# A decoder layer on one core: the whole program in stated TensorE order, norms and token forms as steps between products, inverse root through Ln and Exp

## The chip, the cores and the metric

The kernel runs on 1 core of one Trainium2 chip. A core has five engines that run side by side, each working through its own queue in order: TensorE (PE; matmul), VectorE (DVE), ScalarE (ACT), GpSimd (POOL) and SyncE (SP), which here issues the DMA transfers. The metric is the device time of one launch in microseconds. Time before: 3101.36 us, the median of 3 runs (3099.22 to 3108.59).

## The reference

One step of one decoder layer, width 1024, for 1024 prompt tokens and 8 x 4 sample tokens, 1056 tokens in all. Its norms, where this change works, are one function:

```python
def _rmsnorm(x, g):
    xf = x.astype(jnp.float32)
    y = xf * lax.rsqrt(jnp.mean(xf * xf, axis=-1, keepdims=True) + EPS)
    return (y * g.astype(jnp.float32)).astype(x.dtype)

h = x + 0.5 * _swiglu(_rmsnorm(x, g_ffn1), w_ffn1_in, w_ffn1_out)
u = _rmsnorm(h, g_mix)
# mixer on u: dilated window attention, gated linear attention, cross-attention into
# 256 memory tokens, whose keys and values are
kv = _rmsnorm(mem, g_mem) @ w_mem_kv
h = h + jnp.sum(gates * br, axis=2) @ w_out
h = h + 0.5 * _swiglu(_rmsnorm(h, g_ffn2), w_ffn2_in, w_ffn2_out)
y = _rmsnorm(h, g_final)
```

The reference also returns the new keys and values, the memory keys and values and the states of the linear attention.

## The kernel before, in words

**Products.** Tokens lie along the free dimension, features on the 128 partitions: a [1024, 1056] activation is eight tiles of 128 x 1056. Each fp32 operand is split into a high and a low part, and a product takes three matmuls per tile of the contracted dimension, high by high, high by low, low by high (`product`, L180 to L182). `split` (L186, L187) makes the high part by a cast on ScalarE and the low part by a subtraction on VectorE or GpSimd; `weights` (L166, L167) does the same for weights, in two rotating buffers each (whi, wlo).

**The SwiGLUs.** The hidden width 2816 is worked in 22 blocks of 128. In a block the pair of input products (two weight matrices by two token halves) goes as 7 products in place of 8, with sums and differences of the weights (`weight_forms`) and of the tokens (class `Forms`). The 1056 tokens are four chunks of 264 (c = 0 to 3), in two halves p = 0, 1. Per half and per row of forms i = 0 to 3, `Forms.make` scales four pieces by gain and inverse root (L316), makes two subtractions on GpSimd (L318, L319) and two on VectorE (L320, L321), and splits the results into the tiles xs. `pair_products` then runs j = 0 to 6 for both halves, each product 12 matmuls of 264 columns (4 rows by 3). The token forms are made once, ahead of the first block, for all 22 blocks. The output product (`out_product`) sums over blocks of 4 or 3 hidden tiles: for each of 8 output tiles and 3 chunks of 352 tokens a product of 12 or 9 matmuls, added onto h by VectorE (L554). In the last such block the chunk loop is the outer one, so that the norm of a finished chunk can begin.

**Norms.** Per chunk ScalarE squares (L208) and GpSimd adds (L209); a matmul with ones (L235) sums over partitions and gives one sum per token, on partitions. `rsqrt` (L220 to L227, 13 VectorE operations: a first guess from the bits and three Newton steps) makes rqy. `spread` (L245) brings it back to a row on every partition by matmuls with the identity; `normed` (L255) or the forms (L316) use it.

**The first norm.** `x_features` reads nine tiles of rows, sums their squares on ScalarE and VectorE, transposes them (L435) and copies them out (L439, L441). **Memory.** After the first output block of the first SwiGLU comes `mem_kv`: the 256 memory rows' squares (L475), root, scaling (L481), 16 transposes (L488), then the products for keys and values.

**What sets the order.** A scheduler places the instructions of each engine's queue by its own timing model and by priorities; the norms' sums and spreads have high priority. Only the mixer between the two SwiGLUs runs in a manual TensorE order, the order of the code.

## Time and profile before

| what | value |
|---|---|
| median of 3 runs | 3101.36 us (3099.22 to 3108.59) |
| the profiled execution | 3088.57 us |
| its span, first to last instruction | 3086.8 us |
| TensorE busy | 2917.7 us, 95% |
| VectorE, ScalarE, GpSimd busy | 48%, 33%, 32% |
| mean granted TensorE clock | 0.968 of full |

Busy shares are over the whole span. A table of stretches shows the same for a part of it, a timeline lists single instructions with start and duration in us, and a bracket at the end of its row gives the idle time of the engine ahead of the instruction and what ended it. Matmuls overlap, so that the duration of one is longer than the step from one to the next; the step is read from the evacuations behind products.

### The profile page before, as it was taken

The page shows a single profiled execution, that of the slowest core. Times are in us where ns is not written, and L with a number is a line of the kernel's source. Part 1 is how long each engine was busy: PE and PEld are TensorE (multiplying, and loading weights), DVE is VectorE, ACT ScalarE, POOL GpSimd, SP SyncE. Part 2 cuts the span into 40 slices and gives each one's busy share as a digit, 9 for nine tenths or more (in the row PEclk, how much of TensorE's full clock was granted, in tenths as well). Part 3 has the DMA queues.
Part 4 walks back from the last instruction along what each step waited for, and adds up shares of the span by engine and source line. Part 5 has one row for each costly group of instructions (what it writes and reads, how often), then busy time and mean ns, then how long its engine had stood idle before and what let it go on. Part 6 is the DMA issues. An engine that isn't in the chain of part 4 may idle for free. (4 is left out here: it accounts for less than half of the span.)

```text
span 3086.8 us, 51261 instructions
## 1 busy us (share of the span) xinstructions
PE 2917.7 (95%) x20747; PEld 2843.8 (92%) x20747; DVE 1488.5 (48%) x2746; ACT 1005.5 (33%) x2014; POOL 994.8 (32%) x815
## 2 busy tenths in 40 slices
PE   4999999999999999999898998999995999999998
PEld 3999999899999999988797997999995999999997
DVE  8444444554623446656665551222257444444545
ACT  4333333221435443332232421221224333333212
POOL 5333332010400114546456350222436333332100
PEclk6999999999999999999999999999997999999999
DMA  4222224431311224657566564221221222225312
GB/s 141 76 82 77 84 73 164 145 126 55 106 51 48 71 55 133 174 156 199 143 193 176 169 197 114 70 66 42 98 78 61 83 81 73 83 77 196 104 50 89
DMA packets 438883, 328.65 MB, mean 106 GB/s; under 512 B 34131, under 2 KB 396597, under 8 KB 438645
## 3 DMA queue, kind: packets, MB, share of 16 engines
q1 hardware_dynamic: 438578, 325.35, 34.7%
q8 instruction: 163, 2.67, 0.4%
q14 instruction: 76, 0.61, 0.1%
q10 hardware_dynamic: 66, 0.02, 0.0%
HBM read 264.69 MB, written 60.60 MB: 105 GB/s over the span
## 5 line engine op out<-in xcount | busy, mean ns | idle before, releaser
L180 PE MATMUL acc<-xh,whi 128*128 128x352 f32 x1776 | 594.9, 335 | 0.0
L182 PE MATMUL acc<-xh,wlo 128*128 128x352 f32 x1776 | 583.0, 328 | 8.4 <-DVE wlo L167 8.4
L181 PE MATMUL acc<-xl,whi 128*128 128x352 f32 x1776 | 581.2, 327 | 0.0
L182 PEld LDWEIGHTS acc<-xh,wlo 128*128 128x128 f32 x1776 | 340.7, 192 | 13.9 <-DVE wlo L167 13.9
L180 PEld LDWEIGHTS acc<-xh,whi 128*128 128x128 f32 x1776 | 341.8, 192 | 10.9 <-issue 8.2
L166 ACT CAST whi<-raw 128x512 fp32r<-128x512 f32 (+3 forms) x197 | 157.5, 800 | 569.9 <-PE acc L181 513.1
L181 PEld LDWEIGHTS acc<-xl,whi 128*128 128x128 f32 x1776 | 341.3, 192 | 0.1
L182 PE MATMUL acc<-hh,wlo 128*128 128x352 f32 x960 | 309.1, 323 | 0.8 <-DVE wlo L167 0.8
L181 PE MATMUL acc<-hl,whi 128*128 128x352 f32 x960 | 309.6, 323 | 0.0
L180 PE MATMUL acc<-hh,whi 128*128 128x352 f32 x960 | 309.2, 323 | 0.0
L180 PE MATMUL acc<-xs,swf 128*128 128x264 f32 x1056 | 300.5, 285 | 0.0
L181 PE MATMUL acc<-xs,swf 128*128 128x264 f32 x1056 | 300.3, 285 | 0.0
L182 PE MATMUL acc<-xs,swf 128*128 128x264 f32 x1056 | 300.1, 285 | 0.0
L167 DVE TENSOR_TENSOR wlo<-raw,whi 128x512 fp32r<-128x512 f32 (+3 forms) x197 | 210.8, 1070 | 168.1 <-ACT whi L166 158.2
L554 DVE SCALAR_TENSOR_TENSOR h<-acc,h 128x352 f32<-128x352 f32 x288 | 149.2, 523 | 227.9 <-PE acc L182 227.4
L608 POOL TENSOR_TENSOR u<-u,u 128x264 f32<-128x264 f32 x88 | 66.2, 753 | 514.4 <-ACT u L599 514.4
L180 PE MATMUL acc<-xs,wlo 128*128 128x264 f32 x704 | 200.9, 285 | 2.8 <-ACT u L376 2.4
L181 PE MATMUL acc<-xs,wlo 128*128 128x264 f32 x704 | 200.6, 285 | 0.0
L182 PE MATMUL acc<-xs,wlo 128*128 128x264 f32 x704 | 200.2, 284 | 0.0
L181 PEld LDWEIGHTS acc<-xs,swf 128*128 128x128 f32 x1056 | 199.2, 189 | 0.0
L180 PEld LDWEIGHTS acc<-xs,swf 128*128 128x128 f32 x1056 | 199.1, 189 | 0.0
L182 PEld LDWEIGHTS acc<-xs,swf 128*128 128x128 f32 x1056 | 198.4, 188 | 0.0
(416 smaller groups left out, 6771.5 us busy)
## 6 DMA issues: line engine op xcount, KB each, us to landing
raw<-in_w_ffn_in SPq DMA_DIRECT2D x88, 512.0 KB, 3.8
raw<-in_w_in SPq DMA_DIRECT2D x52, 512.0 KB, 4.1
kq<-sqt SPq DMA_DIRECT2D x96, 256.0 KB, 4.7
hraw<-hidd SPq DMA_DIRECT2D x44, 528.0 KB, 4.5
raw<-in_w_ffn_out SPq DMA_DIRECT2D x64, 256.0 KB, 2.9
kq<-in_cache_swa SPq DMA_DIRECT2D x64, 256.0 KB, 5.5
vc<-in_cache_swa SPq DMA_DIRECT2D x64, 256.0 KB, 4.9
raw<-in_w_gate SPq DMA_DIRECT2D x24, 512.0 KB, 3.8
```

Of the source, the lines that this page charges most:

```text
L166: nc.scalar.copy(hi[:, :n], raw[:, :n])
L167: nc.vector.tensor_sub(lo[:, :n], raw[:, :n], hi[:, :n].bitcast(F32))
L180: mm(ps, wh[k], xh[k], start=first and k == 0, stop=False, skip_group_check=more)
L181: mm(ps, wh[k], xl[k], start=False, stop=False, skip_group_check=more)
L182: mm(ps, wl[k], xh[k], start=False, stop=last and k == n - 1, skip_group_check=more)
L554: nc.vector.scalar_tensor_tensor(hv, ps, scale, hv, op0=ALU.mult, op1=ALU.add)
L608: nc.gpsimd.tensor_mul(add, second[p], add)
```

## The change

- The whole program is built under the manual TensorE order, not the mixer alone. What is to stand between products is held as generators in a queue, `later`; `step` runs one of them to its next `yield` after a product, `finish` runs out what is left.
- The inverse root is Ln and Exp on ScalarE and one Newton step of 4 VectorE operations.
- A chunk's norm (`norm_steps`) puts the sum and root four steps after the chunk's last tile and the spread one product later. The mixer's first stage (`gla_begin`) takes two steps after each of its products and finishes what is left.
- Token forms are made per chunk (`Forms.half`). The scaled pieces overwrite h in the second SwiGLU and have two tiles of their own in the first; the low part of the last form (xs3) is made on VectorE, of one of the two first forms (xs0) on GpSimd.
- In the first block of each SwiGLU the seven products of the first half go ahead of those of the second (`apart`). The first SwiGLU's rows 0 to 4 are loaded, transposed and normed first; the rest is steps between the first products, and the store of x follows there.
- The memory keys and values are steps between the products of the first output block and those after.
- h behind w_out is stored by chunks, 32 stores in place of 8. The last block's transposes and sums of squares follow two products late (`lag`). Which of the weight forms lie in the rotating buffers changes (the first and third in whi, the second and fourth in wlo).

```diff
+    def step(self):
+
+        while self.later:
+            try:
+                next(self.later[0])
+                return
+            except StopIteration:
+                self.later.popleft()
...
-        v, y, t = (self.small(f"rq{i}", n) for i in "vyt")
-        nc.vector.tensor_scalar(v, ssq, 1.0 / D, EPS, op0=ALU.mult, op1=ALU.add)
-        nc.vector.tensor_scalar(t.bitcast(I32), v.bitcast(I32), 1, None, op0=ALU.logical_shift_right)
-        nc.vector.tensor_scalar(y.bitcast(I32), t.bitcast(I32), -1.0, float(0x5f3759df), op0=ALU.mult, op1=ALU.add)
-        nc.vector.tensor_scalar(v, v, -0.5, None, op0=ALU.mult)
-        for _ in range(3):
-            nc.vector.tensor_mul(t, y, y)
-            nc.vector.tensor_mul(t, t, v)
-            nc.vector.scalar_tensor_tensor(y, t, 1.5, y, op0=ALU.add, op1=ALU.mult)
+        y, t = (self.small(f"rq{i}", n) for i in "yt")
+        nc.scalar.activation(y, ssq, AF.Ln, bias=self.eps, scale=1.0 / D)
+        nc.scalar.activation(y, y, AF.Exp, scale=-0.5)
+        nc.vector.tensor_mul(t, y, y)
+        nc.vector.scalar_tensor_tensor(t, ssq, D * EPS, t, op0=ALU.add, op1=ALU.mult)
+        nc.vector.tensor_scalar(t, t, -0.5 / D, 1.5, op0=ALU.mult, op1=ALU.add)
+        nc.vector.tensor_mul(y, y, t)
...
+    def norm_steps(self, ssq, then):
+
+        yield
+        yield
+        yield
         with self.tc.high_priority():
             y = self.rsqrt(self.token_ssq(ssq))
-            return self.spread([(y[:, i:i + 1], a, b) for i, (_, a, b) in enumerate(pieces(ssq.shape[1]))])
-
-    def norm_chunk(self, h, c, ssq, g, x):
-        self.normed(h, c, self.token_rows(ssq), g, x)
+        yield
+        with self.tc.high_priority():
+            r = self.spread([(y[:, i:i + 1], a, b) for i, (_, a, b) in enumerate(pieces(ssq.shape[1]))])
+        then(r)
...
-    def make(self, p, h, r, g):
+        self.column = {}
+
+    def half(self, c, h, r, g, in_place):
 
 
         k, nc = self.k, self.k.nc
+        p, second = c // 2, c % 2
+        if in_place:
+            x = [h[kk][:, cs(c, 4)] for kk in range(KD)]
+        else:
+            two = [k.slab("xn"), k.slab("xn")]
+            x = [two[kk % KH // 2][:, (kk % 2 * 2 + kk // KH) * HC:(kk % 2 * 2 + kk // KH + 1) * HC] for kk in range(KD)]
         for i in range(KH):
-            a, b = k.slab("xfa"), k.slab("xfb")
-            slot = [(b if j > 3 else a)[:, j % 4 * HC:(j % 4 + 1) * HC] for j in range(8)]
-            x11, x21, t2, t1, t3, t4, x22, x12 = slot
-            for x, kk, c in ((x11, i, 0), (x12, i, 1), (x21, i + KH, 0), (x22, i + KH, 1)):
-                nc.vector.scalar_tensor_tensor(x, h[kk][:, cs(2 * p + c, 4)], g[:, kk:kk + 1], r[c],
+            for kk in (i, i + KH):
+                nc.vector.scalar_tensor_tensor(x[kk], h[kk][:, cs(c, 4)], g[:, kk:kk + 1], r,
                                                op0=ALU.mult, op1=ALU.mult)
+            if not second:
+                t = k.slab("xs0", F32R)
+                self.three[p][i] = [t]
+                for j in range(2):
+                    k.split(t[:, j * HC:(j + 1) * HC], t[:, (j + 2) * HC:(j + 3) * HC], x[i + j * KH],
+                            nc.gpsimd if j else nc.vector)
+        if not second:
+            self.first = x
+            return
+        n = 2 * HC
+        for i in range(KH):
+            x11, x21, x12, x22 = self.first[i], self.first[i + KH], x[i], x[i + KH]
+            a = k.slab("xt")
+            t2, t1, t3, t4 = (a[:, j * HC:(j + 1) * HC] for j in range(4))
             nc.gpsimd.tensor_sub(t1, x12, x11)
             nc.gpsimd.tensor_sub(t3, x22, x12)
             nc.vector.tensor_sub(t2, x22, t1)
             nc.vector.tensor_sub(t4, x21, t2)
-            s = self.three[p][i] = [k.slab(f"xs{j}", F32R) for j in range(3)]
+            s = [k.slab(f"xs{j}", F32R) for j in (1, 2)]
+            self.three[p][i] += s
             if i % 2 == 0:
                 self.last[p][i // 2] = k.slab("xs3", F32R)
-            two = self.last[p][i // 2][:, i % 2 * 2 * HC:(i % 2 + 1) * 2 * HC]
-            n = 2 * HC
+            two = self.last[p][i // 2][:, i % 2 * n:(i % 2 + 1) * n]
             k.split(s[0][:, :n], s[0][:, n:], a[:, :n], nc.vector)
             k.split(s[1][:, :n], s[1][:, n:], a[:, n:], nc.gpsimd)
-            k.split(s[2][:, :n], s[2][:, n:], b[:, :n], nc.vector)
-            k.split(two[:, :HC], two[:, HC:], x22, nc.gpsimd)
+            k.split(two[:, :HC], two[:, HC:], x22, nc.vector)
...
+    for n in range(14):
+        j, p = (n % 7, n // 7) if apart else (n // 2, n % 2)
...
+        k.step()
...
+            if f % 4 == 3:
+                yield
...
+            r = k.spread([(x.column[i], max(t0 - i * 128, 0), min(t1 - i * 128, rows[i].shape[0]))
+                          for i in range(t0 // 128, (t1 - 1) // 128 + 1)])
+        x.half(c, h, r, g, False)
+        yield
...
     r = k.rsqrt(ms2)
     for i, xi in enumerate(xt):
         nc.vector.tensor_scalar(xi, xi, r[:, i:i + 1], None, op0=ALU.mult)
+    yield
+    yield
...
         k.split(hi[f // 4][:, f % 4:f % 4 + 2], lo[f // 4][:, f % 4:f % 4 + 2], xn, nc.vector)
+        yield
...
         w = k.weights(wv[:, :, h * E:(h + 1) * E], KD, E)
+        yield
...
+            hv = h[n][:, cs(c, 4)]
+            with k.tc.high_priority():
+                k.nc.sync.dma_start(hd[n * 128:(n + 1) * 128, cs(c, 4)], hv)
+            k.squares(ssq, hv, n == 0)
             if n == KD - 1:
-                rows[c] = k.token_rows(ssq)
-                if c % 2:
-                    x.make(c // 2, h, [rows[c - 1], rows[c]], g)
+                k.later.append(k.norm_steps(ssq, lambda r: x.half(c, h, r, g, True)))
...
+            told.append((after, n))
+            if len(told) > lag:
+                f, m = told.popleft()
+                f(m)
+            k.step()
...
+        if b == 0 and filler:
+            k.later.append(filler())
         if b < len(blocks) - 1:
             out_product(k, hid, blk, wo, h, 0.5)
-            if b == 0 and filler:
-                filler()
         else:
-            out_product(k, hid, blk, wo, h, 0.5, after_chunk=after_chunk)
+            k.finish()
+            out_product(k, hid, blk, wo, h, 0.5, after_chunk=after_chunk, lag=lag)
...
+    rows = x_rows(k, range(5))
     raw0 = [k.raw_weights(v, KD, 128) for v in ffn_view(A["w_ffn1_in"][0], 0)]
+    rows += x_rows(k, range(5, NB + 1))
...
+    def second():
+        yield from x_features(k, rows, h0, g_ffn1, x, 1)
+        store_h(0, h0)
+
+    h0 = h
+    k.later.append(second())
...
-            build(ctx, tc, A, O)
+            with tc.manual_schedule(engines={mybir.EngineType.PE}):
+                build(ctx, tc, A, O)
```

How this moves instructions, at three places. TensorE in the first SwiGLU's first output block, where `ident,mem` marks the memory rows' transposes, hh and hl the hidden tiles, mh and ml the normed memory. Before:

```order
L182 MATMUL acc<-hh,wlo 128x352
L488 MATMUL aux<-ident,mem 128x128 x16
L180 MATMUL acc<-mh_6207,whi 128x256 x2
L181 MATMUL acc<-ml_6209,whi 128x256
L182 MATMUL acc<-mh_6207,wlo 128x256
```

and after, where these transposes stand behind 36 of the block's matmuls:

```order
L195 MATMUL acc<-hl,whi 128x352
L196 MATMUL acc<-hh,wlo 128x352
L521 MATMUL aux<-ident,mem 128x128 x4
L194 MATMUL acc<-hh,whi 128x352
L195 MATMUL acc<-hl,whi 128x352
```

Before, the 16 transposes followed the block's 288 matmuls together; now they come in four groups, the first after three products and the others one product apart.

TensorE at the norms behind w_out (mh, ml: the merged branches; swh, swl, whi, wlo: w_out; `ones,ssq`: the sums; `ident,rqy`: the spread). Before, at the end of that product, with the third and fourth chunks' spreads:

```order
L180 MATMUL acc<-mh_21418,whi 128x264
L181 MATMUL acc<-ml_21426,whi 128x264
L182 MATMUL acc<-mh_21418,wlo 128x264
L245 MATMUL aux<-ident,rqy 128x128
L235 MATMUL aux<-ones,ssq 128x1 x3
L245 MATMUL aux<-ident,rqy 128x128
L245 MATMUL aux<-ident,rqy 128x8
L245 MATMUL aux<-ident,rqy 128x128 x2
L245 MATMUL aux<-ident,rqy 128x8
L180 MATMUL aux<-xs_22245,whi 128x264
```

and after, for the first chunk (the second and third have the same rows one chunk on):

```order
L246 MATMUL aux<-ones,ssq 128x1 x3
L194 MATMUL acc<-mh_21383,swh 128x264
L195 MATMUL acc<-ml_21391,swh 128x264
L196 MATMUL acc<-mh_21383,swl 128x264
L194 MATMUL acc<-mh_21384,swh 128x264
L195 MATMUL acc<-ml_21392,swh 128x264
L196 MATMUL acc<-mh_21384,swl 128x264
L194 MATMUL acc<-mh_21385,whi 128x264
L195 MATMUL acc<-ml_21393,whi 128x264
L196 MATMUL acc<-mh_21385,wlo 128x264
L256 MATMUL aux<-ident,rqy 128x128 x2
L256 MATMUL aux<-ident,rqy 128x8
```

One product now stands between a chunk's sum and its spread. The fourth chunk's pair lies in the second SwiGLU's first block, around the second of its products on the form xs1. At the first norm behind the first SwiGLU the rows are alike with 352 columns; for its third chunk the spread follows the sum directly.

ScalarE at the memory rows' norm. Before, squares among weight casts, the root on VectorE:

```order
L166 CAST whi<-raw 128x512
L475 ACTIVATE mjunk,mms<-mem 128x512 x2
L166 CAST whi<-raw 128x512
L475 ACTIVATE mjunk,mms<-mem 128x512 x2
L166 CAST whi<-raw 128x512 x4
```

and after:

```order
L180 CAST whi<-raw 128x512
L506 ACTIVATE mjunk,mms<-mem 128x512 x4
L233 ACT_TABLE_LOAD
L233 ACTIVATE rqy<-mms_5825,eps 128x2
L234 ACT_TABLE_LOAD
L234 ACTIVATE rqy<-rqy 128x2
L200 CAST mh_5865<-mxn 128x512 x2
```

The root has moved to ScalarE's queue, behind the squares, with a table load ahead of each of its two functions; the next weight cast stands behind the casts of the normed memory.

## Rows read from the trace of the kernel before

**Rows 1.** The page's first part: TensorE's busy time, share of the span, instructions.

```profile
PE 2917.7 (95%) x20747; PEld 2843.8 (92%) x20747; DVE 1488.5 (48%) x2746; ACT 1005.5 (33%) x2014; POOL 994.8 (32%) x815
```

**Rows 2.** Stretches: length, busy us (instructions) of each engine, clock, DMA share, GB/s.

```profile
0.00:77.00 77.00, 35.12 (x144) 28.86 (x145) 65.78 (x138) 34.21 (x77) 41.49 (x52) 0.65 0.41 141
...
570.00:630.00 60.00, 53.18 (x321) 48.42 (x319) 33.70 (x50) 24.71 (x32) 11.84 (x5) 0.97 0.58 188
...
2300.00:2380.00 80.00, 47.23 (x318) 44.45 (x317) 63.69 (x130) 33.46 (x68) 52.27 (x49) 0.74 0.21 76
2380.00:2900.00 520.00, 519.43 (x4079) 519.01 (x4078) 240.23 (x380) 187.17 (x384) 173.09 (x132) 1.00 0.31 99
2900.00:3087.00 187.00, 172.55 (x1096) 171.17 (x1094) 91.50 (x187) 38.38 (x76) 7.42 (x3) 0.98 0.24 77
```

**Rows 3.** Tile rqy on TensorE: idle us and times until VectorE's L227.

```profile
  DVE rqy L227: 39.0, 4
```

**Rows 4.** Timeline of VectorE, last root: start us, us, line, operation.

```profile
3076.93 0.17 DVE L220 TENSOR_SCALAR rqv<-ysum 128x3 f32<-128x3 f32 x1
...
3079.11 0.16 DVE L227 SCALAR_TENSOR_TENSOR rqy<-rqt,rqy 128x3 f32<-128x3 f32 x1
```

**Rows 5.** Timeline of ScalarE, a Ln and Exp pair of the mixer.

```profile
983.80 1.28 ACT L194 ACT_TABLE_LOAD   x1
985.10 0.29 ACT L194 ACTIVATE rs_y<-aux,eps 128x32 f32<-128x32 f32 x1
985.40 1.28 ACT L195 ACT_TABLE_LOAD   x1
986.69 0.23 ACT L195 ACTIVATE rs_y<-rs_y 128x32 f32<-128x32 f32 x1
```

**Rows 6.** Matmuls on the token forms xs in two stretches: length, busy (count), clock.

```profile
0.00:77.65 77.65, 13.50 (x50) 0.65 0.42 143
...
2314.00:2361.20 47.20, 11.26 (x42) 0.57 0.16 59
```

**Rows 7.** Timeline of VectorE, evacuations of two successive products behind w_out.

```profile
2282.42 0.43 DVE L554 SCALAR_TENSOR_TENSOR r<-acc,r 128x264 f32<-128x264 f32 x1 [0.66 <-PE acc L182]
2283.51 0.43 DVE L554 SCALAR_TENSOR_TENSOR r<-acc,r 128x264 f32<-128x264 f32 x1 [0.65 <-PE acc L182]
```

**Rows 8.** Timeline of VectorE: first sum of squares, first forms, last split of a form.

```profile
11.24 0.16 DVE L446 TENSOR_TENSOR xsq<-xsq 128x5 f32<-128x5 f32 x1
...
25.98 0.89 DVE L316 SCALAR_TENSOR_TENSOR xfa<-x,gain_cols,aux 128x264 f32<-128x264 f32 x2 [0.92 <-PE aux L245]
...
72.51 1.83 DVE L187 TENSOR_TENSOR xs<-xfb,xs 128x528 fp32r<-128x528 f32 x1
```

**Rows 9.** Timeline of GpSimd, one row of forms: two subtractions, a split.

```profile
2338.61 0.75 POOL L318 TENSOR_TENSOR xfa<-xfb,xfa 128x264 f32<-128x264 f32 x1 [5.26 <-DVE xfb L316]
2339.31 1.22 POOL L319 TENSOR_TENSOR xfb<-xfb 128x264 f32<-128x264 f32 x1
2341.57 1.30 POOL L187 TENSOR_TENSOR xs<-xfa,xs 128x528 fp32r<-128x528 f32 x1 [1.04 <-ACT xs L186]
```

**Rows 10.** Timeline of VectorE, first output block: two evacuations, scaled memory rows.

```profile
526.16 0.53 DVE L554 SCALAR_TENSOR_TENSOR h<-acc,h 128x352 f32<-128x352 f32 x1 [1.50 <-PE acc L182]
528.08 0.53 DVE L554 SCALAR_TENSOR_TENSOR h<-acc,h 128x352 f32<-128x352 f32 x1 [1.39 <-PE acc L182]
...
543.88 1.41 DVE L481 TENSOR_SCALAR mem<-mem,rqy 128x1024 f32<-128x1024 f32 x2
```

**Rows 11.** Timeline of ScalarE, last square of the memory rows.

```profile
536.79 0.62 ACT L475 ACTIVATE mjunk<-mem 128x512 f32<-128x512 f32 x1
```

**Rows 12.** Waits of TensorE from 800 to 870: us, times, longest.

```profile
PE acc L182 <- DVE wlo L167: 3.3, 1, 3.3
```

**Rows 13.** Timeline of VectorE, first and last step of third chunk's root.

```profile
2309.58 0.15 DVE L220 TENSOR_SCALAR rqv<-aux 128x3 f32<-128x3 f32 x1
...
2329.10 0.69 DVE L227 SCALAR_TENSOR_TENSOR rqy<-rqt,rqy 128x3 f32<-128x3 f32 x1
```

More of the change, by code (lines that the diff above doesn't have):

```diff
@@ new lines, in x_features @@
+    at = range(0, 5) if p == 0 else range(5, NB + 1)
+    sq = k.small("xsq", 10)
+    nc.gpsimd.memset(sq, 0.0)
+    for i in at:
+        xt, n, c = rows[i], rows[i].shape[0], i - at[0]
+        half = xt[:, :512]
+        nc.scalar.activation(k.t512("xjunk")[:n], half, AF.Square, accum_out=sq[:n, c:c + 1])
+        half = xt[:, 512:]
+        nc.vector.tensor_tensor_reduce(k.t512("xjunk")[:n], half, half, 1.0, 0.0, ALU.mult, ALU.add,
+                                       sq[:n, 5 + c:6 + c])
@@ new lines, in x_features @@
+    sq2 = k.small("xsq2", 5)
+    with k.tc.high_priority():
+        nc.vector.tensor_add(sq2, sq[:, 0:5], sq[:, 5:10])
+        y = k.rsqrt(sq2)
+    for i in at:
+        x.column[i] = y[:rows[i].shape[0], i - at[0]:i - at[0] + 1]
+    for at0, at1 in ((0, 4), (4, 5)) if p == 0 else ((5, 8), (8, 9)):
+        for f in range(KD):
+            ps = k.aux() if f % 2 else k.acc()
+            w = 0
+            for i in range(at0, at1):
+                n = rows[i].shape[0]
+                nc.tensor.transpose(ps[:, w:w + n], rows[i][:, f * 128:(f + 1) * 128], k.ident[:n, :n])
+                w += n
+            dst = h[f][:, at0 * 128:at0 * 128 + w]
+            if f % 2:
+                nc.vector.tensor_copy(dst, ps[:, :w])
+            else:
+                nc.scalar.copy(dst, ps[:, :w])
+            if f % 4 == 3:
+                yield
@@ L571, in out_product @@
             evac(ps, n, c)
-            after(n)
+            told.append((after, n))
+            if len(told) > lag:
+                f, m = told.popleft()
+                f(m)
+            k.step()
+    for f, m in told:
+        f(m)
 def ffn_view(w_in, j):
```

135 lines of the change are left out of this document (52 added, 83 removed).

## The prediction

> **What bounds the kernel now.** Read the page's first part first: TensorE is busy 2917.7 us, 95% of the span [rows 1]. Only its waits are to be had, so the next view is the table by stretches. Between the stage borders there is nothing: the second SwiGLU's input products keep TensorE busy 519.43 of 520 us at full clock [rows 2]. The idle time lies at the borders: 41.9 us of the first 77, 6.8 us of 570 to 630, 32.8 us of 2300 to 2380, 14.4 us of the last 187 [rows 2]. In two of these TensorE also runs at mean clocks of 0.65 and 0.74 of its 2.4 GHz; that is, for much of the time at 1.2 GHz [rows 2]. Third, ask who ended the waits: four waits, 39.0 us in all, ended when VectorE had the inverse root rqy ready for the matmul that spreads it over the partitions [rows 3]. The mixer (some 930 to 2260 us) keeps its order and is left out.
>
> **The change part by part.** Sums are made in the profiled execution, 3088.57 us, 12.8 us below the median 3101.36; I add a difference to the median.
>
> *The inverse root.* It was 13 VectorE operations; undisturbed, the first starts at 3076.93 and the last ends at 3079.27, 2.3 us [rows 4]. It becomes Ln and Exp on ScalarE and 4 VectorE operations. The pair exists in the kernel before: each function has a table load of 1.28 us ahead of it, and 128x32 takes 0.29 and 0.23 us [rows 5]. Four dependent VectorE steps of 0.2 us [rows 4] add 0.8. So 0.29 + 1.28 + 0.23 + 0.8 and some 0.3 for two handovers is 2.9 us where Ln's table is in before the sum arrives, 4.2 us where ScalarE comes late and loads it then. Alone it is longer than before; it is better only where VectorE is full, since 9 operations leave that queue.
> The Trainium skill ("ScalarE: Activation LUTs", "Table sets: the hidden batching unit") says that ln then exp needs one load, as one set has both, at about 2.7 us. The trace shows two loads per pair at 1.28 us; the measurement decides. By the page's figure for both loads each root would be some 2.8 us longer, by its one set 1.3 us shorter than mine.
>
> *Start.* Before, 50 of the first block's matmuls (2 halves x 7 products x 12 = 168) are recorded by 77.65 us [rows 6]; the other 118 at 0.121 us (nine 264-column matmuls take 1.09 us [rows 7]) end the block at 91.9. The token forms run on VectorE from 25.98 to 74.3 [rows 8] with both roots' 26 operations among them. The first sum of squares is there at 11.4 in either kernel [rows 8]; the first half's root now ends 4.2 us later, with some 6 us for transposes' copies between its steps and the five spreads the first form starts at about 21.7. Sixteen scalings at 0.44 us (two take 0.89 [rows 8]) are 7 us. Then POOL sets the pace: per row of forms two subtractions and a split, 0.75 + 1.22 + 1.30 = 3.3 us [rows 9], four rows 13 us, so the half is ready at about 43. The second half's spreads stand behind five and six of the first half's products, about 50 to 53; 7 + 13 us more and weight work give 72 to 76. What cannot start before the last row of forms is 51 of 84 matmuls, 6.2 us at full clock, 11 at half: end at 78 to 87, I take 84, **-8**. Bounds: -15 with all at full clock and no queueing; +3 if transposes' copies behind the forms on VectorE hold TensorE, whose order is now fixed.
>
> *Memory keys and values.* TensorE used to reach the memory rows' transposes after the whole block of 24 output products; now after 3. A product takes 1.92 us [rows 10], so with the block's first at 524.2 it is there at 530.0. The rows are loaded behind the eight h rows and their last square starts at 536.79 [rows 11]: done at 537.4. Then the sum 0.2, a root with Ln's table behind the squares on ScalarE 4.2, the scaling 1.41 [rows 10]: about 543. TensorE waits 13 us, where before this work was hidden under products. In exchange the separate memory stretch goes, 6.8 us idle and 1.8 lost to half clock (a clock of 0.97 over 60 us [rows 2]). The wait also costs a spell of half clock, 1.8 by the same row. Behind the waiting transposes stand all further h products; their evacuations and the next weight casts wait with them. Sum 13 + 1.8 - 8.6 = 6.2, with 2 for weight buffers that h and memory products now share: **+8**, bounds +2 (rows land 4 us earlier) and +14 (no exchange for the buffer waits).
>
> *Norm between first SwiGLU and mixer.* Before, the order put some five products between a sum and its spread, at no idle time. Now one product of nine 352-column matmuls (9/12 of 1.92, 1.44 us) covers a root of 2.9 to 4.2: 1.5 to 2.8 us of wait, twice. The third chunk's spread follows its sum with nothing between: 2.9 to 4.2. Together 5.9 to 9.8, and up to 1.8 each for half clock. Against that stands a wait of 3.3 us for low weight halves [rows 12], behind VectorE's root operations; I count 2 of it as saved. **+7**, bounds +1 and +13.
>
> *Norm between mixer and second SwiGLU.* Before, the third chunk's root starts at 2309.58 and ends at 2329.8 between form operations [rows 13]; TensorE stands for it, and only 42 of 168 matmuls are recorded by 2361.2 [rows 6]: block end 2361.2 + 126 x 0.121 = 2376.4. Now its four VectorE steps take 3 to 4 us even between form operations. But a product here is only 1.09 us [rows 7], so each of the first three chunks waits 2 to 3 us, the third longer because POOL's sums of squares queue among the form subtractions. Last product about 2325 (2314 before, where the stretch in [rows 6] starts), fourth spread 2333, eight scalings and four rows of forms, 3.5 + 13 us, behind it to 2350, 51 matmuls and some half clock to 2357 to 2372: I take 2367, **-9**; bounds -18 and +3, the latter if POOL's queue holds the third sum 10 us.
>
> *Tail and rest.* The last root has nothing above it: 4.2 for 2.3, +1.9; transposing two products later saves short waits of the last block, some 1 us: **+1**, bounds -2 and +3. Storing h2 in 32 pieces, two other forms in the rotating weight buffers, x rows in two parts: hidden under stretches with TensorE full, **0**, bounds -1 and +3 if a weight buffer comes free late in one block of the 22.
>
> Sum: -8 + 8 + 7 - 9 + 1 = -1 us: about 3101 on the median.
>
> **The rivals.**
> *Faster.* The borders' idle goes as intended. For it: 39.0 us of TensorE's idle time have one cause [rows 3], and VectorE is busy 63.7 of 80 us at the second border [rows 2], so 36 fewer operations count there. Start and mid at their good ends, -15 - 18, the norms and memory at +4 each: -25, 3076. Against it: the forms' volume on VectorE and POOL is the same.
> *Slower.* One mechanism: the fixed spacing of one product between sum and spread. Each of the seven sums leaves TensorE standing, and every stop drops it to 1.2 GHz, as after the 6.8 us in 570 to 630. With Ln's table loaded behind the sum at each: 7 x (1.3 + 1.8) = 22 us on the sum above: 3123. It decides when ScalarE still holds casts or squares when the sum arrives. Against it: at the second border TensorE waits for forms anyhow, so perhaps four of the seven count (+12, 3113).
> The Trainium skill ("Perfetto Trace Analysis", "Matmul Optimizations") says that TensorE's power scales with use and matmuls should run back to back in batches; that is against steps of single products. This trace agrees at the borders (0.65 and 0.74).
> *No effect.* The stated order changes nothing since forms set both ends as before and only memory and norms pay: +16 less what the tail keeps, 3115; part of slower.
>
> **How the numbers follow.** A measurement of this kernel tells no change from 0.3%, 9.3 us: 3092.1 to 3110.7. The sum's likely error is the two borders (about 8 each) and memory and norms (about 6 each), together some 14. No measurable change, 3101 (own range 3092 to 3111): 0.40. Faster 0.32, slower 0.28 (the spacing 0.18, no effect 0.10). For 8 in 10 I reach past the faster case (3076, itself uncertain by some 10) and to the slower one: 3069 to 3123.
>
> **What would show it.** Right: a wait of 10 to 15 us before the first memory transposes, no idle around 570 to 630's work, waits of 1.5 to 4 us before each of the norm's spreads, the first product of the second SwiGLU at least 5 us earlier, two table loads in every root. Wrong: memory transposes without a wait; spreads without waits (then the faster case); first form not before 25 us, or first block still ending near 92; half clock in long stretches where it was full.

## The result and the profile after

The changed kernel takes 3128.04 us in the median of 4 runs (3125.36 to 3136.01), the kernel before 3101.06 us in the median of 4. The ratio is 1.0087 with a 95% interval of 1.0061 to 1.0112. It is slower by about 27 us, where the prediction had no measurable change, 3101 us; the time lies above the range too.

The page's first part of the kernel after, which answers to [rows 1]:

```profile
PE 2939.3 (94%) x20747; PEld 2861.2 (92%) x20747; DVE 1434.7 (46%) x2645; ACT 1052.1 (34%) x2082; POOL 975.4 (31%) x815
```

TensorE has the same 20747 matmuls, and they take 21.6 us more, 9.1 of it in the mixer; the rest of the loss is idle time. The profiled execution is 3125.95 us, its span 3124.2.

To see where both went, the two traces are cut at the same pieces of work. The ten stretches of the trace are: start (to the 168th matmul of the first block of the first SwiGLU), the other input products of the first SwiGLU (to the first matmul on hh, the hidden tiles), memory (to the 576th matmul on them: the first two output blocks with the memory products), output products (to the 1368th), norm (the last output block and the mixer's first products, to the 300th matmul on xh), mixer (to the first matmul on mh in w_out), w_out (its first 432 matmuls), the second border or mid (the last 216 of w_out and the four chunks' norms, to the 168th matmul on the forms of the second SwiGLU), its other input products, and the tail.

The table by stretches of the kernel before, four of the ten rows (length, busy us with instructions of TensorE, its weight loads, VectorE, ScalarE, GpSimd, then clock, DMA share, GB/s): start, memory, norm, mid.

```profile
0.00:92.82 92.82, 50.33 (x264) 43.85 (x265) 72.12 (x149) 41.33 (x92) 47.10 (x56) 0.71 0.38 127
...
524.03:651.93 127.90, 121.08 (x745) 116.30 (x744) 67.11 (x113) 38.45 (x55) 16.84 (x8) 0.99 0.50 164
...
778.65:870.95 92.30, 89.00 (x555) 87.08 (x554) 49.64 (x109) 34.01 (x68) 35.04 (x36) 0.98 0.28 88
...
2284.28:2378.26 93.98, 61.21 (x434) 58.43 (x433) 73.24 (x159) 38.32 (x80) 60.66 (x60) 0.78 0.18 64
```

The same of the kernel after, in order, without the output products and the tail.

```profile
0.00:94.05 94.05, 52.80 (x265) 44.88 (x266) 75.01 (x140) 48.61 (x108) 47.62 (x59) 0.73 0.39 133
94.05:522.94 428.89, 428.89 (x3532) 428.89 (x3531) 178.45 (x312) 166.66 (x356) 148.03 (x123) 1.00 0.28 85
522.94:666.59 143.65, 123.43 (x745) 117.94 (x744) 66.13 (x104) 42.11 (x59) 17.10 (x9) 0.94 0.47 151
...
793.75:897.56 103.81, 93.05 (x554) 90.61 (x554) 44.00 (x82) 43.01 (x80) 36.89 (x36) 0.95 0.25 79
897.56:2248.79 1351.23, 1287.53 (x8820) 1231.20 (x8819) 604.84 (x1193) 425.55 (x847) 463.26 (x369) 0.96 0.41 118
2248.79:2318.75 69.96, 66.91 (x432) 66.32 (x432) 29.75 (x45) 14.70 (x26) 26.28 (x26) 1.00 0.43 140
2318.75:2417.72 98.97, 67.32 (x434) 63.91 (x433) 68.75 (x132) 52.53 (x105) 58.95 (x63) 0.79 0.18 60
2417.72:2847.26 429.54, 429.54 (x3531) 429.54 (x3529) 179.00 (x312) 166.79 (x356) 147.42 (x123) 1.00 0.28 84
```

Read length first, then length less busy time of TensorE, which is its idle time. Memory is 15.8 us longer: idle 20.2 in place of 6.8. Norm is 11.5 longer: idle 10.8 in place of 3.3, and 4.1 us more busy time for the same matmuls, at a mean clock of 0.95 in place of 0.98. Mid is 5.0 longer: idle is 1 us less, but the same 434 matmuls take 6.1 us more. The start is 1.2 longer and w_out 2.9 (67.0 before). The two stretches of input products are 2.3 and 2.2 shorter (431.2 and 431.7 before), the output products are 0.4 longer, the tail 0.1. Without the mixer that makes 32.4 us, which lies inside the interval of the ratio (19 to 35 us). The mixer was 1346.3 us in the first trace of before and 1362.8 in a second one (below), so 1351.2 says nothing of the change.

The table of waits of TensorE after, by stretch: engine, line and tile, what it waited for, us in all, times, longest. From 524.5 to 665.6:

```profile
PE aux L521 <- DVE mem L512: 13.4, 2, 13.3
PE acc L196 <- DVE wlo L181: 2.6, 2, 2.0
PE acc L194 <- ACT whi L180: 2.1, 3, 1.0
PE acc L195 <- DVE wlo L181: 1.6, 2, 1.3
```

The first row is the wait for the memory rows that was forecast. The others are 6.3 us of waits for the high and low parts of weights, about as much as all of TensorE's idle time in this stretch before.

From 790 to 895, and from 2250 to 2430 (of the latter the first and third row):

```profile
PE aux L256 <- DVE rqy L238: 8.6, 3, 4.0
PE acc L196 <- DVE wlo L181: 2.2, 2, 1.9
```

```profile
PE aux L256 <- DVE rqy L238: 20.2, 4, 9.7
...
PE acc L195 <- POOL ml L201: 2.0, 1, 2.0
```

In the kernel before, the waits for the root in mid (2300 to 2380) were these:

```profile
PE aux L245 <- DVE rqy L227: 19.7, 2, 15.8
```

The tile rqy on TensorE over the whole trace after, idle us and times until the last step of the root, as in [rows 3]:

```profile
  DVE rqy L238: 29.9, 8
```

It was 39.0 us in four. The waits became more and shorter. At the start they are nearly gone (1.2 us, 19.4 before), where TensorE now waits for parts of the token forms instead (27.5 us, 10.9 before); in mid they are as long in all as before (20.2 us in four, 19.7 in two); and there are now waits at the norm before the mixer, where none stood.

Why the wait is long is seen in the timeline of the second border, at the first of its roots, first ScalarE (without Ln and Exp themselves), then VectorE:

```profile
2322.89 0.43 ACT L222 ACTIVATE sq<-r 128x264 f32<-128x264 f32 x1 [0.67 <-DVE r L591]
2323.34 1.28 ACT L233 ACT_TABLE_LOAD   x1
...
2324.91 1.28 ACT L234 ACT_TABLE_LOAD   x1
```

```profile
2326.44 0.16 DVE L235 TENSOR_TENSOR rqt<-rqy 128x3 f32<-128x3 f32 x1 [3.64 <-ACT rqy L234]
...
2326.79 0.42 DVE L591 SCALAR_TENSOR_TENSOR r<-acc,r 128x264 f32<-128x264 f32 x1
...
2327.32 0.16 DVE L238 TENSOR_TENSOR rqy<-rqy,rqt 128x3 f32<-128x3 f32 x1
```

From the table load (2323.34) to the last step (2327.48) the root takes 4.1 us, a product only 1.09 [rows 7]. VectorE's first step waits 3.64 us for Exp, and the evacuation L591 stands behind it in the queue. Both table loads come after the square, as the longer of the two prices in the prediction had it (4.2 us). The third chunk's root meets more in ScalarE's queue:

```profile
2362.17 0.26 ACT L233 ACTIVATE rqy<-aux,eps 128x3 f32<-128x3 f32 x1
2362.33 0.62 ACT L200 CAST xs<-xt 128x528 fp32r<-128x528 f32 x1
2362.85 0.72 ACT L200 CAST xs<-r 128x264 fp32r<-128x264 f32 x2
2363.59 1.28 ACT L234 ACT_TABLE_LOAD   x1
2364.89 0.20 ACT L234 ACTIVATE rqy<-rqy 128x3 f32<-128x3 f32 x1
```

Between Ln and Exp stand three casts of token forms and the table load. This is the wait of 9.7 us, the longest of the four.

### The profile page after: what moved, and what is told of

Its sections match the earlier page's. It is cut to its first block, busy times and chain, and to the rows that moved or that the text cites. A ratio compares the mean times of both kernels' runs of the same rounds, so it can differ in the third digit from the quotient of the medians.

```text
span 3124.2 us, 51558 instructions
## 1 busy us (share of the span) xinstructions
PE 2939.3 (94%) x20747; PEld 2861.2 (92%) x20747; DVE 1434.7 (46%) x2645; ACT 1052.1 (34%) x2082; POOL 975.4 (31%) x815
## 4 chain that ended last, share of the span: by engine, by line
PE 77%; DVE 7%; DMA 7%; ACT 3%; issue 2%; POOL 2%; SPq 1%; DVEq 0%; POOLq 0%; ACTq 0%
PE acc L194 22%; PE acc L196 22%; PE acc L195 22%; DVE wlo L181 1%; PE aux L196 1%; PE aux L194 1%; PE aux L195 1%; DMA sd<-stat 1%; DMA kq<-in_cache_swa 1%; DVE xs L201 1%; POOL mqb L1113 1%; DMA cb<-cd 1%; DMA mqb<-mqt 1%; DMA mkc<-in_cache_mem_kv 1%; PE aux L914 1%
## 5 line engine op out<-in xcount | busy, mean ns | idle before, releaser
L591 DVE SCALAR_TENSOR_TENSOR h<-acc,h 128x352 f32<-128x352 f32 x288 | 149.8, 523 | 230.7 <-PE acc L196 230.2
L194 PE MATMUL acc<-xs,whi 128*128 128x264 f32 x704 | 203.4, 289 | 18.9 <-ACT xs L200 17.3
L195 PE MATMUL acc<-xs,whi 128*128 128x264 f32 x704 | 204.8, 291 | 17.1 <-DVE xs L201 17.1
L196 PE MATMUL acc<-xs,whi 128*128 128x264 f32 x704 | 201.9, 287 | 0.7 <-DVE whi L201 0.7
L380 POOL TENSOR_TENSOR ws<-raw 128x512 f32<-128x512 f32 x44 | 59.0, 1340 | 418.7 <-DMA raw<-in_w_ffn_in 413.5
```

Of the source, the lines that this page charges most:

```text
L194: mm(ps, wh[k], xh[k], start=first and k == 0, stop=False, skip_group_check=more)
L195: mm(ps, wh[k], xl[k], start=False, stop=False, skip_group_check=more)
L196: mm(ps, wl[k], xh[k], start=False, stop=last and k == n - 1, skip_group_check=more)
L380: nc.gpsimd.tensor_add(s1, b1, b2)
L591: nc.vector.scalar_tensor_tensor(hv, ps, scale, hv, op0=ALU.mult, op1=ALU.add)
```

## The experiments

Two theories stood at first. By the theory of the order the stated order is the cause: a short dependent piece (sum, root, spread; memory rows) stands at a fixed distance of too little work, TensorE stops there and then runs at the lower of its two clocks. By the theory of the root the new root is the cause, through ScalarE's table loads. (The expectations number their own theories A, B and C anew for each run.) The ratios are to the kernel before, measured beside the run.

### The kernel before, once more

No edit; 

> The kernel before, once more. Theory (the traces differ by 37.4 us where the medians differ by 27, since the profiled execution of before lay 12.8 us under its median): a second trace of before is 8 to 15 us longer than the first, and the difference lies in the mixer (930 to 2250 us), whose order neither kernel changes; start, memory, norms and second SwiGLU agree within 1 us with the first trace. Rival: the stages around the change vary as much from run to run, so that stage differences under 5 us say nothing.

Measured: 3101.52 us (10 runs) against 3098.69 (19), ratio 1.0017 (1.0001 to 1.0033). Its row for the mixer:

```profile
869.95:2232.77 1362.82, 1291.28 (x8821) 1233.93 (x8819) 612.89 (x1193) 426.57 (x848) 461.98 (x369) 0.96 0.41 117
```

The first trace had 1346.3 us here. All other stretches agree within 0.8 us between the two traces. So stretches of single traces can be compared to within about a microsecond, save the mixer's; that the first profiled execution lay 12.8 us under the median is, by these two traces, the mixer's doing. The ratio is a measure of the noise too: one and the same kernel came out at 1.0017, with an interval that just leaves out 1.

### The old root in the new kernel

```diff
-        nc.scalar.activation(y, ssq, AF.Ln, bias=self.eps, scale=1.0 / D)
-        nc.scalar.activation(y, y, AF.Exp, scale=-0.5)
...
+        for _ in range(3):
+            nc.vector.tensor_mul(t, y, y)
+            nc.vector.tensor_mul(t, t, v)
+            nc.vector.scalar_tensor_tensor(y, t, 1.5, y, op0=ALU.add, op1=ALU.mult)
```

> The changed kernel with the 13-operation inverse root on VectorE put back. Theory A (in steps of one product the chain sum, table load, Ln, table load, Exp, four VectorE steps sets the wait): VectorE's own root is 2.3 us alone, so the waits of 2.3, 2.3 and 4.0 us at the first norm and 3.5, 3.5 and 3.5 at the second fall to 1 or 2 us each, the wait of 13.3 us at the memory rows by 2; 10 to 14 us less in all, about 3115. Rival B (forms and rows set the ends, the kind of root does not matter): within 4 us of the changed kernel, 3124 to 3132. Rival C (the root stretches in VectorE's full queue, as it did before): the wait of 9.7 us at the third chunk behind w_out grows to 15 and more, in all 3130 or above.

Measured: 3126.02 us (4 runs), ratio 1.0097 (1.0068 to 1.0126). Waits of TensorE from 2318 to 2420, the first two rows:

```profile
PE aux L259 <- DVE rqy L241: 10.1, 4, 2.8
PE aux L249 <- POOL ssq L223: 8.5, 2, 7.7
```

Waits for the root halve (20.2 to 10.1), but the sum of the third chunk now comes 7.7 us late from GpSimd, and the stretch is as long as it was (99.3 us against 99.0). The 10 to 14 us that theory A of this expectation forecast did not come; the time is that of its rival B. The theory of the root falls: with either root the kernel is as slow.

### The new root in the kernel before

```diff
-        nc.vector.tensor_scalar(v, ssq, 1.0 / D, EPS, op0=ALU.mult, op1=ALU.add)
...
+        nc.scalar.activation(y, ssq, AF.Ln, bias=self.eps, scale=1.0 / D)
+        nc.scalar.activation(y, y, AF.Exp, scale=-0.5)
```

> The kernel before with the Ln and Exp root alone. Theory A: where several products stand between sum and spread the longer chain is hidden and VectorE is freed; the third chunk's root behind w_out no longer takes 20 us, the first block of the second SwiGLU ends 5 to 12 us earlier, the start 2 to 5 us; 7 to 15 us less than before, 3086 to 3094. Rival B (VectorE's and POOL's volume of form operations sets both ends): within 4 us of before. Rival C (ScalarE's in-order queue holds casts and squares behind the waiting Ln): 5 us or more slower than before.

Measured: 3094.36 us (10 runs) against 3098.69, ratio 0.9975 (0.9958 to 0.9993). The start and mid are each 2.7 us shorter (90.1 and 91.3), the norm is 1.0 shorter, memory 1.9 and the tail 2.6 longer. Outside the mixer the trace is 1.3 us shorter in all (1739.2 against 1740.5). So where the scheduler chooses the order, the short root alone is worth little: 4.3 us by the medians, near the 2.8 by which the same kernel missed itself, and the 7 to 15 of theory A did not come.

### Memory steps begun later

```diff
+            def behind(g):
+                for _ in range(8):
+                    yield
+                next(g)
+                for _ in range(6):
+                    yield
+                yield from g
+            k.later.append(behind(filler()))
```

> The changed kernel with the memory steps begun later: squares, root and scaling of the memory rows after 8 products of the first output block, transposes some 8 products after that; all else as in the changed kernel. Theory A (the wait of 13.3 us for the rows is nearly the whole loss of that stage): no wait ahead of the memory transposes, the stage (first to 576th matmul on hidden tiles) 13 to 15 us shorter, in all about 3114. Rival B (sharing weight buffers between output and memory products costs the same again wherever the steps stand): the stage is only 5 to 8 us shorter, 3120 to 3123.

Measured: 3131.65 us (4 runs), ratio 1.0112 (1.009 to 1.0134). The wait of 13.3 us is gone, but the stretch is 142.1 us, 1.6 less: idle time is 13.8 us, and the matmuls take 128.3 us at a mean clock of 0.92 (123.4 at 0.94 in the kernel after). TensorE waits 8.3 us for parts of weights and 5.5 for parts of hidden tiles. One cast of a hidden tile on ScalarE, and SyncE's queue ahead of it:

```profile
584.90 1.07 ACT L200 CAST hh<-hraw 128x1056 fp32r<-128x1056 f32 x1 [5.57 <-DMA hraw<-hidd]
```

```profile
577.37 0.32 SPq L538 DMA_DIRECT2D ktd<-mkt  x1
579.78 0.38 SPq L166 DMA_DIRECT2D raw<-in_w_mem_kv  x1
580.20 0.58 SPq L665 DMA_DIRECT2D hraw<-hidd  x1
```

The load of this hidden tile (580.20) stands in SyncE's queue behind a store of memory keys (577.37), for which the queue waits 5.1 us until ScalarE has copied them, and a load of memory weights (579.78), for which it waits 2.0 us until VectorE has read the buffer that it goes into. My reading is that this sharing of one queue is part of the cost; no run tests it by itself, and ScalarE's waits for hidden tiles in the stretch (27.7 us in ten) were as long in the kernel before (28.5 in eleven). What the run shows is that moving the wait did not remove the stretch's cost; my forecast that it would, failed.

### More distance between sum and spread

```diff
         yield
+        yield
+        yield
         with self.tc.high_priority():
             r = self.spread(
```

> The changed kernel with three products in place of one between a chunk's sum and its spread, at both norms. Theory A (the fixed spacing of one product sets these waits): the first norm's stage (103.8 us, 92.3 in the kernel before) loses its first two waits of 2.3 us and their half clock and comes to 95 to 98; behind w_out the first two waits of 3.5 us go and the third of 9.7 becomes 5 or less, the stage to the 168th form product comes from 99.0 to 88 to 92. Rival B (the forms' volume on VectorE and POOL sets the second stage's end): the waits go there too, but the stage stays within 3 us of 99.0; only the first norm gains.

Measured in one run: 3114.78 us, 13.3 less than the median after (the kernel before is at 3100.9 beside it). The norm and mid (the fifth and eighth rows of its table):

```profile
795.69:891.27 95.58, 89.96 (x554) 87.31 (x554) 44.87 (x81) 42.19 (x80) 36.68 (x36) 0.98 0.26 85
...
2314.36:2406.47 92.11, 64.41 (x435) 59.53 (x434) 70.67 (x132) 51.74 (x105) 59.80 (x64) 0.85 0.20 65
```

The norm goes from 103.8 to 95.6 us, its mean clock back to 0.98; mid from 99.0 to 92.1, the clock from 0.79 to 0.85. All other stretches but the mixer stay within 1.4 us. TensorE's waits for the root fall from 29.9 to 8.0 us. This is the theory of the order, for the norms: two products more between sum and spread are worth 15 us.

### Memory products on their own

```diff
-            k.later.append(filler())
+            memory = filler()
+            def rows_only():
+                for _ in range(8):
+                    yield
+                next(memory)
+            k.later.append(rows_only())
...
+            if b == 0 and filler:
+                k.finish()
+                for _ in memory:
+                    pass
```

> The changed kernel with the memory products as a stretch of their own behind the first output block, as before; the rows' squares, root and scaling after 8 products of that block. Theory A (it is the interleaving, by weight buffers and hidden tiles that wait in one queue, and not only the wait for the rows, that costs): the memory stage comes from 143.7 back to 127 to 130 us (127.9 before; 142.1 with the steps begun later). Rival B (the stated order itself costs there, since the scheduler no longer fills gaps of the memory stretch with output products): 133 to 140.

Measured in one run: 3123.37 us. The memory stretch, and the waits of TensorE in it:

```profile
523.25:654.14 130.89, 121.60 (x746) 117.30 (x744) 62.26 (x104) 41.48 (x59) 17.34 (x9) 0.97 0.51 168
```

```profile
PE aux L542 <- ACT mkt L537: 5.1, 4, 1.3
PE acc L195 <- DVE ml L201: 3.0, 1, 3.0
```

143.7 us become 130.9; before it was 127.9. Rows, squares and root run under output products, and the products stand in one piece, as in the kernel before. What is left is four waits of 1.3 us for the copy of the keys ahead of their transposes, and one for ml that the kernel before had as well (2.9 us). The total falls by less: the norm is 2.6 us longer in this run and w_out 1.6, which no run explains, and the mixer 5.0.

### The start in two steps

```diff
-            if f % 4 == 3:
+            if f == KD - 1 and at1 - at0 > 1:
                 yield
```

> The changed kernel with the second half's transposes in two steps in place of four, so that its spreads stand behind the second and third product and not the fifth and sixth. Theory A (the second half's forms start late, at 58.3 us, because their spreads queue behind products that wait for the first half's forms): they start by 46 to 50, the 168th form product comes from 94.0 to 84 to 89. Rival B (VectorE and POOL are full of forms either way): within 2 us of 94.0.

Measured in one run: 3128.77 us. The start is 89.8 us, 4.2 less; the mixer of this run is 7 us longer than that of the run after, so the total shows nothing. The second half's first scaling comes at 51.4 us in place of 58.3, and the forecast was 46 to 50, with 84 to 89 for the start. So the transposes of the second half of the rows, put between the first products in four steps, held the first block back by some 4 us, and most of the start's length has another cause.

### The three together

The three edits above in one kernel. 

> The last three edits together (wider spacing, memory products apart, second half's spreads earlier). If each holds by its theory A: 8 + 15 + 7 + 9 = 39 us under the changed kernel, about 3090, 10 under the kernel before. If only the memory edit holds: about 3113.

Measured: 3101.22 us (10 runs) against 3100.9, ratio 1.0005 (0.9987 to 1.0023). Start 90.4, memory 130.5, norm 96.8, mid 93.4 us. Three changes of where the steps stand bring the 27 us back. The forecast was 39 us: start, memory, norm and mid give 29.5.

### The same, with the transposes of the keys a product later

```diff
-        pt = k.aux()
...
+        kts.append(kt)
+        if h:
+            turn(h - 1)
```

> The changed kernel with wider spacing, memory products apart, second half's spreads earlier (3101.2 us in the run before this), and in addition each head's transposes of the memory keys behind the next head's product, since TensorE waited four times 1.3 us for the copy ahead of them. Theory A: the four waits go, with their half clock, memory stage from 130.5 to 124 to 127 us, about 3096. Rival B: the wait moves to the weights of the next product, stage within 1.5 us of 130.5.

Measured: 3096.24 us (10 runs) against 3095.54, ratio 0.9999 (0.9983 to 1.0014). Memory is 128.2 us, 2.2 less than without the edit, and as before the change; that lies between the two forecasts, and in the total it is too little to be told.

### The stated order in the mixer alone

```diff
+    with tc.manual_schedule(engines={mybir.EngineType.PE}):
+        Mix(k, u[0], od, ktd, vd, g_gla).run()
+        m = gated_branches(k, u[0], od, (1, 2, 0))
...
-            with tc.manual_schedule(engines={mybir.EngineType.PE}):
-                build(ctx, tc, A, O)
+            build(ctx, tc, A, O)
```

> The changed kernel with the stated TensorE order taken back to the mixer alone: same code (short root, token forms by halves, steps, weight buffers), but a scheduler sets TensorE's order outside the mixer. Theory A (what costs is the stated order with its fixed spacings; the new pieces by themselves gain): memory stage 127 to 131 us (143.7 with the stated order), first norm 91 to 94 (103.8), the stage behind w_out to the 168th form product 86 to 93 (99.0), start 85 to 92 (94.0); about 3090, some 10 under the kernel before. Rival B (the pieces themselves, forms by halves and other engines for the splits, cost): start and second stage stay at 93 to 99, about 3100.

Measured: 3082.44 us (10 runs) against 3095.54, ratio 0.9957 (0.9941 to 0.9974), faster than either kernel. Start and the input products behind it, then memory, norm, mid and the input products behind mid:

```profile
0.00:75.50 75.50, 51.46 (x264) 43.90 (x265) 63.67 (x128) 42.14 (x98) 42.43 (x53) 0.77 0.46 159
75.50:512.87 437.37, 433.69 (x3530) 432.22 (x3530) 193.94 (x325) 171.84 (x368) 156.59 (x129) 0.99 0.27 84
512.87:643.18 130.31, 122.86 (x745) 118.96 (x744) 65.23 (x104) 41.45 (x59) 16.76 (x8) 0.96 0.50 166
...
769.90:866.55 96.65, 89.64 (x555) 88.08 (x554) 42.66 (x81) 42.02 (x79) 36.16 (x36) 0.96 0.26 84
...
2292.96:2367.81 74.85, 62.20 (x435) 58.63 (x434) 61.20 (x121) 46.94 (x97) 55.93 (x58) 0.85 0.21 69
2367.81:2805.34 437.53, 434.27 (x3530) 433.13 (x3529) 190.67 (x325) 171.28 (x365) 154.98 (x128) 0.99 0.27 85
```

Idle time of TensorE at the start is 24.0 us (42.5 before, 41.3 after), in mid 12.7 (32.8 and 31.7). Part of it is given back, since work is moved over the borders: the input products behind them are 6 us longer than before. Start with what is behind it is 512.9 us against 524.0 before and 522.9 after; mid with what is behind it 512.4 against 525.7 and 528.5. Outside the mixer the trace is 1722.1 us, 18.4 less than before (1740.5) and 50.8 less than after (1772.9): the stated order costs these pieces 50.8 us, and the pieces by themselves, the new root among them, gain 18.4.

They don't gain everywhere. The norm before the mixer stays 4.4 us longer than in the kernel before (96.7 against 92.3; the forecast was 91 to 94), and memory 2.4. The tile rqy on TensorE over the whole trace:

```profile
  DVE rqy L238: 4.6, 1
```

This one wait is the third chunk's at that norm. In mid TensorE no longer waits for the root at all (20.2 us with the stated order); what is left there are waits for the forms. How the order differs is seen in the timeline of TensorE in this run (start us, us, line, tiles):

```profile
54.62 0.52 PE L194 MATMUL aux<-xs,wlo 128*128 128x264 f32 x1
54.94 0.48 PE L194 MATMUL acc<-xs,swf 128*128 128x264 f32 x1
...
57.41 0.42 PE L196 MATMUL acc<-xs,swf 128*128 128x264 f32 x1
57.63 0.42 PE L195 MATMUL aux<-xs,wlo 128*128 128x264 f32 x1
```

A product into aux is left after a matmul, a whole product of 12 matmuls into acc is worked, and then the first goes on. In the stated order a product that waits for its next form holds all that stand behind it (waits of 1.9, 2.6 and 1.7 us between 42 and 49 us in the kernel after). So the theory of the order holds in a wider form than I had put it: besides the distances it is the order of matmuls and whole products at the two borders. How the gain of this run divides between the two is not shown.

### Which part of that gain is the root

The kernel of the last run with the old root, and again as it was, on one chip. The first edit is the one shown at the old root above.

> The changed kernel with the stated order in the mixer alone, as in the run before, and with the 13 VectorE operations of the old inverse root; what is left of the change is the token forms by halves, the rows, memory and norms as steps, placed by the scheduler. If the gain of that run came from the forms by halves, this one stays 5 to 10 us below the kernel before (ratio 0.997 to 0.998), the first stretch near 78 and the one before the second SwiGLU near 78 us, both some 3 us longer than with the short root (75.5 and 74.9). If the gain was the short root's alone (its ratio alone was 0.9975), this one is back at the kernel before, 0.999 to 1.001, with both stretches near 90.

> The same kernel as the run with the stated order in the mixer alone, a second time, on the same chip as the one with the old root, so that the two differ by the root alone. If both parts add, 0.995 to 0.997 of the kernel before and 5 to 9 us below the one with the old root. If the root is worth nothing where the scheduler places the products, within 3 us of it.

Measured: with the old root 3087.6 us (12 runs), ratio 0.996 (0.9946 to 0.9975); as it was 3079.38 us (9 runs), ratio 0.9948 (0.993 to 0.9967); the kernel before 3098.8. So the new forms, rows and steps are worth some 11 us with the old root, where the scheduler places them, and the root some 8 more by the medians; the two intervals overlap, and the same kernel gained 13 and not 19 in the run above, so by the times the root's share is not sure. By the traces outside the mixer, which repeat better, the kernel before has 1740.5 us, this one with the old root 1731.9, with the new one 1723.8 and, above, 1722.1. By stretches of the two traces the new root is worth 4.9 us at the norm (102.7 to 97.8), 2.8 in mid (77.6 to 74.8) and 3.2 behind it, and costs 2.3 in the tail (273.8 to 276.1). At the norm before the mixer the new pieces with the old root cost 10.4 us (102.7, 92.3 in the kernel before), even where the scheduler places them. The start is the same with either (75.2 and 75.5): my forecast of 3 us there was wrong.

## Why the prediction was wrong

The sum was -1 us and the time rose by 27. Against the first trace, without the mixer, the stretches rose by 32.4. Of the signs that the prediction named, the wait before the memory transposes, the waits before the spreads and the two table loads came. The first block still ends near 92 (94.1), a sign of being wrong; memory idles beside its wait; and the second SwiGLU's first product is not 5 us earlier but 2.4 later in its stretch (56.0 us into mid, 53.6 before). Step by step, with the effect at a border and in the input products behind it taken together:

- **The inverse root** came as worked out: two table loads of 1.28 us each in every root, 4.1 us in all where Ln's table is loaded behind the sum, as at the second border. The Trainium skill ("ScalarE: Activation LUTs", "Table sets: the hidden batching unit") has one load for ln then exp; the rows above show two. As a mechanism it did not decide: the old root in its place leaves the kernel as slow.
- **The start, -8 forecast, -1.1 found** (+1.2, and -2.3 behind it). The first form started at 22.5 us as forecast (21.7). The second half is where the step failed: its spreads stand at 56.1 and 57.7 us instead of 50 to 53, behind products that wait for forms of the first half, and its forms end not 20 but 28 us behind the first scaling at 58.3, with the last low part on VectorE at 85.2. I had priced a row of forms by GpSimd's 3.3 us [rows 9] and given VectorE's other work some 2 us in all; but it makes low parts of weights in between, and on it one and the same subtraction (L353) takes 0.43 us at 77.41 and 1.42 at 79.16. The faster rival was right about the pieces: placed by the scheduler they take 11 us off the start and what is behind it.
- **Memory, +8 forecast, +15.8 found.** The wait of 13.3 us was forecast at 13. The credit of 8.6 us against it, for the separate memory stretch that was to go, did not come: TensorE still idles 6.8 us in the stretch beside that wait, most of it for parts of weights. Outside the credit the sum was 13 + 1.8 + 2 = 16.8.
- **Norm before the mixer, +7 forecast, +11.5 found.** Waits of 2.3, 2.3 and 4.0 us before spreads came as described, 8.6 in all within my 5.9 to 9.8. Of the 3.3 us of waits for low weight halves [rows 12] 2.2 are still there, so 1.1 are saved in place of 2. Too small was the lower clock: 4.1 us of extra busy time, of which about 1 stood in the +7. 8.6 - 1.1 + 4.1 makes 11.6, the 11.5 but for rounding. Part of it is not the stated order: 4.4 us stay where the scheduler places the same pieces.
- **Norm before the second SwiGLU, -9 forecast, +2.8 found** (+5.0, and -2.2 behind it). This is the step that failed most. I let four VectorE steps of the third chunk end in 3 to 4 us, so that the 15.8 us wait of the kernel before would go. It took 9.7 us of TensorE's time, the longest wait of the norms, and the other three waits of 3.5 us make 20.2, where 19.7 stood. The timeline above shows Ln at 2362.17 and Exp at 2364.89 with three casts of forms and a table load between them on ScalarE, and VectorE has the steps from 2365.12 to 2367.12 with form operations between them. I had seen that the root leaves VectorE's queue and not what it meets in ScalarE's. The idle time as a whole went down by 1 us all the same; what made the stretch longer is 6.1 us of extra busy time at the lower clock (107 of its matmuls stand over 0.2 us behind the one before, 55 before the change), which I had named ("some half clock") and not priced.
- **w_out, 0 forecast, +2.9 found:** a wait of 2.0 us for the low part ml from GpSimd (in the answer above) and one of 1.0 for low weight halves, in a stretch where I had everything hidden; with the scheduler's order it is 67.0 again.
- **Tail and rest, +1 forecast, +0.1 and +0.4 found.** The last root's own part, forecast at 1.9, is 2.3 between the last two runs; the rest of the tail gives as much back: in the changed kernel with the old root the tail is 273.9, 2.9 less than in the kernel before.

The rival on the slower side, fixed spacing of one product between sum and spread, names the mechanism that the run with three products shows: some 15 of the 27 us. The prediction gave it a chance of 0.18 and a time of 3123, on a sum that held the memory credit; without that credit of 8.6 us it would have been some 3132, and the time lies between the two. That is in part luck: the same sum held -8 and -9 for the two borders, which did not come either.

## What to carry to other kernels

A stated order on an in-order engine turns each short dependent chain into a wait unless the distance in it is as long as the chain at its worst, casts and table loads on the other engines included: measure that chain end to end and put that many products between. Price the clock with the wait: at the norm the 7.5 us of added idle time cost another 4.1 in slower matmuls. And separate what a change adds from how it is placed: outside the mixer the new pieces gain 8.6 us with the old root and 17 to 18 with the new one, and the stated order took 50.8 away.

## What the runs showed of the hardware

A wait can have an echo: in mid after the change, idle time was 1 us less than before and the stretch 5 us longer, the same 434 matmuls being busy 67.3 us in place of 61.2. The mean clock of the stretch does not tell it (0.79 and 0.78), since it also counts the idle time (the kernel after has a mean clock of 0.60 in 530 to 543 us, with TensorE busy for 0.7 of the 13); the busy time of the same matmuls does.

The stretch of the mixer took 1346.3 and 1362.8 us in two traces of one kernel (the one before), and 1359.4 and 1351.6 in two of another (the stated order in the mixer alone), while the other stretches of these pairs repeat within 1.2 us. A difference of 10 us between two single traces can be this alone.
